# A decoder block on one core: value blocks a weight part later, a latent weight chunk ahead of the queries, the FFN input turned ahead of the last output product

## The chip, the cores and the metric

The kernel runs on one core of a Trainium2 chip. A core has five engines that run side by side, each through its own queue in order: PE (TensorE, matmuls and transposes into PSUM), DVE (VectorE), ACT (ScalarE), POOL (GpSimd) and SP (SyncE, which here issues nearly all loads). The metric is the device time of one execution in microseconds, as a median of several.

## What is computed

One block of a transformer: two token mixers side by side, then a feed-forward network (FFN), for 512 tokens of width 1024, all float32. The reference, cut to what matters:

```python
mod = silu(c) @ ada_w + ada_b                      # six rows of 1024: shifts, scales, gates
h = rms_norm(x, norm1_gain) * (1 + sc1) + sh1
z = h @ w_in                                       # 1024 -> latents, q, k/v of three branches, gates
c_q, c_kv, k_pe, q_n, k_c, v_c, k_s, v_s, k_w, v_w, g_nsa, g_mla, g_merge = split(z)
q  = rms_norm(c_q) @ w_q_b;  kv = rms_norm(c_kv) @ w_kv_b        # latent attention, 8 heads
y_mla = causal_attention(q, k, v) @ w_o_mla
# sparse attention: keys and values of 31 overlapping blocks of 32 tokens,
# compressed by a small network; selected blocks; a window of 256
def compress(t, pos_emb, w1, w2):
    flat = (t[:, blk_idx] + pos_emb).reshape(..., CMP_LEN * Dh)
    return silu(flat @ w1) @ w2
kc, vc = compress(k_c, ...), compress(v_c, ...)
y_nsa = (gated sum of compressed, selected and window attention) @ w_o_nsa
x = x + gt1 * ((sigmoid(g_mla) * y_mla + sigmoid(g_merge) * y_nsa) @ w_out)
h2 = rms_norm(x, norm2_gain) * (1 + sc2) + sh2
x = x + gt2 * ((silu(h2 @ ffn_w_gate) * (h2 @ ffn_w_up)) @ ffn_w_down)
```

## The kernel before

Every product of float32 values is made of three matmuls on halves: a value `v` is split into a rounded high part (`..hi`, `..h`) and the rest (`..lo`, `..l`), and `hi*hi + hi*lo + lo*hi` is summed in PSUM. ACT makes the high half (`hi_of`), DVE the low one (`lo_of`). So each loaded weight chunk (`raw`, loaded by SP) becomes `whi` on ACT, then `wlo` on DVE, and then feeds PE. The pool `wp` has four buffers each of `raw`, `whi` and `wlo`. In PSUM there are four buffers `mm` for sums, two `sc` and two `tp` (transposes and small results).

All engines are wrapped in `Paced`, whose line 153 issues nearly every instruction; that is why the trace gives L153 almost everywhere and instructions are told apart by their tiles. Three things set the order. While `Paced.strict` is true (from line 514 to 1233) every instruction of an engine follows the one written before it, so the written order is the order on the chip. Behind that, a scheduler orders the instructions by its own plan of times, within the dependences. And `gate` on a wrapped engine ties what is issued to follow a given earlier instruction of that engine.

The work goes through these stages, with their times in the trace: modulation strips and the first products (0 to 60 us), the strict part with the rest of `w_in` up to the latents (60 to 148), sparse attention (to 292), latent projections (to 340), latent attention (to 430), gated output products (to 456), the out product `wo` (to 502), the FFN (to 864).

Many steps are generators; `steps(g, n)` runs the next n pieces of one, `run(g)` all of it, `mix` interleaves several by their numbers of pieces, and `with_side` runs one while filler work (gate products, modulation sums) is issued at its side. Three places are touched.

*Lines 1179 to 1201, strict.* `feed.prep(n)` splits the weight chunks up to number n and issues loads four further. `cols_products(j)` multiplies all four token tiles by two of the eight k rows of a part of 352 columns (24 matmuls `ga`); four of these calls make a group, and `keep_cols` copies the group's four sums to `zA`, tiles 0 and 2 on ACT, 1 and 3 on DVE. The next group's sums need the PSUM buffers that these copies free. Between them stand: `blocks["v"]` (`compress_blocks`, line 854), which transposes the value columns `ZC` into `pt`, copies them to `X` (three copies on ACT, one on DVE) and makes, in two halves, `FF` (DVE), its high part `FS` (ACT) and its low part `FS` (DVE); `w1["v"]` (`compress_w1`), four pieces of products `ph` from `FS`; the key side's `nk`, `pk`, `outs["k"]` (`po`, `kcr`, `kcd`, `KH`, `KL`); and `mods_gen` (`mods`, line 1000), pieces of a sum over strips of `ada_w`: a strip is loaded into a single buffer `strip`, and two DVE instructions add its two rows into `macc`.

*Line 1532.* The queries' first half is made token tile by token tile (`tok_major`, tiles `gq`), each tile's result copied to `qn` and squared into `jq` on ACT (`use_q`), and mixed with `kv_chunk(1)`, the load and split of the second chunk of `mla_w_kv_b`, which the products `gk` behind it need.

*Lines 1765 to 1767.* `out_pairs` makes the out product's last two pairs of token tiles in ten pieces; in the second five, `make_h2(0)` is mixed, which scales the first two token tiles to `xs`, and then for each pair of k rows transposes them into `pt`, makes `h2h`, `h2f` and `h2l` (the FFN's input, halves). The FFN's first products `fg` (gate) and `fu` (up) need these; `first_gate_up` goes on with the second half, `make_h2(1)`.

Of the kernel before, what the change touches and what calls it, by code (L numbers as in the profile page):

```python
# [116 lines left out]
def hybrid_block(ctx, tc, a, out):  # L117
# [47 lines left out]
    pe, act, dve, pool, sp = (Paced(e) for e in (nc.tensor, nc.scalar, nc.vector, nc.gpsimd, nc.sync))  # L165
# [149 lines left out]
    def run(gen):  # L315
        for _ in gen:
            pass

    def steps(gen, n):
        for _ in range(n):  # L320
            if next(gen, "end") == "end":
                break
# [20 lines left out]
    def mix(*pairs):  # L343
        todo = [[g, n, 0] for g, n in pairs if n]
        while todo:
            best = min(todo, key=lambda e: (e[2] + 0.5) / e[1])
            if next(best[0], "end") == "end":
                todo.remove(best)
            else:
                best[2] += 1  # L350
                yield
# [18 lines left out]
    def with_side(gen):  # L370
        for _ in gen:
            side.tick()
# [220 lines left out]
    def hA(k, t):  # L593
        return hT[k][0][:, t * P : (t + 1) * P], hT[k][1][:, t * P : (t + 1) * P]
# [20 lines left out]
    def use_q(t, ps):  # L615
        act.activation(out=UQ[t].rearrange("p h d -> p (h d)"), in_=ps, func=AF.Copy)
# [441 lines left out]
    mods_gen = mods()  # L1058
# [4 lines left out]
    blocks, w1, w2, outs = ({nm: f(i, nm) for i, nm in (K, V)} for f in (compress_blocks, compress_w1, compress_w2, compress_out))  # L1063
# [87 lines left out]
    def cols_products(j):  # L1151
        h, l = feed.take(order.index(cols_a[j]))
        if j % 4 == 0:
            gemm["ps"] = [mm.tile([P, S], F32, name=f"ga{t}", tag="mm")[:, :352] for t in range(NT)]
        for i in range(2):
            k = 2 * (j % 4) + i
            for t in range(NT):
                ah, al = hA(k, t)
                o = gemm["ps"][t]
                pe.matmul(o, ah, h[:, i, :], start=(k == 0), stop=False)  # L1160
                pe.matmul(o, ah, l[:, i, :], start=False, stop=False)
                pe.matmul(o, al, h[:, i, :], start=False, stop=(k == KD - 1))

    def keep_cols(j):
        for t in range(NT):
            use_a(352 * j)(t, gemm["ps"][t])
# [12 lines left out]
    steps(outs["k"], 1)  # L1179
    steps(tq, 1)  # L1180
    cols_products(2)
    steps(blocks["v"], 1)
    feed.prep(19)
    steps(blocks["v"], 1)
    steps(mods_gen, 2)
    cols_products(3)
    steps(outs["k"], 1)
    keep_cols(0)
    steps(outs["k"], 1)
    feed.prep(20)  # L1190
    steps(blocks["v"], 1)
    cols_products(4)
    feed.prep(21)
    steps(blocks["v"], 1)
    steps(mods_gen, 2)
# [2 lines left out]
    steps(nk, 1)  # L1198
    steps(w1["v"], 1)
    feed.prep(23)  # L1200
    cols_products(6)
    steps(pk, 1)
    feed.prep(24)
    steps(w1["v"], 1)
# [215 lines left out]
    with tc.tile_pool(name="mp", bufs=1, side="right", reuse_waits="tile") as mp:  # L1420
# [16 lines left out]
        def chunks(w, kt, c0, n, got):  # L1437
            for k0 in range(0, kt, 2):
                got.append(wchunk(rows(a[w][0], k0 * P, 2, c0, n), 2, n))
                yield  # L1440

        def tok_major(off, kt, n, got, consume, tag):
            for t in range(NT):
                ps = mm.tile([P, S], F32, name=f"g{tag}{t}", tag="mm")[:, :n]
                for k in range(kt):
                    ah, al = (v[:, t * P : (t + 1) * P] for v in cT[off + k])
                    h, l = (v[:, k % 2, :] for v in got[k // 2])
                    pe.matmul(ps, ah, h, start=(k == 0), stop=False)
                    pe.matmul(ps, ah, l, start=False, stop=False)
                    pe.matmul(ps, al, h, start=False, stop=(k == kt - 1))  # L1450
                    if k % 3 == 2:
                        yield
                consume(t, ps)
                yield

        wk, wq = [[], []], [[], []]
        kv_chunk = lambda c: chunks("mla_w_kv_b", 2, 512 * c, 512, wk[c])
# [37 lines left out]
        def norm_q(c):  # L1495
            hs = slice(4 * c, 4 * c + 4)
            dve.scalar_tensor_tensor(out=msq[:, c], in0=msq[:, c], scalar=1.0 / MQK, in1=each_t(vq, 4), op0=ALU.mult, op1=ALU.add)
            rsqrt(flat(rsq[:, c]), flat(msq[:, c]), mt, f"q{c}", pool)
            yield
# [29 lines left out]
        za_st.close()  # L1529
        qk_st = scope()  # L1530
        qkp = qk_st.enter_context(tc.tile_pool(name="qkp", bufs=2, reuse_waits="tile"))
        with_side(mix((tok_major(0, 6, 384, wq[0], use_q(0), "q0"), 12), (kv_chunk(1), 1)))
        run(norm_q(0))
        with_side(mix((tok_major(6, 2, 512, wk[1], use_kv(1), "k1"), 4), (q_chunks(1), 3)))
        qk = [[] for _ in range(NH)]
# [225 lines left out]
    wo = gemm_tok(mA, a["w_out"][0], KD, 0, S, use_o(0), tag="wo0")  # L1761
# [2 lines left out]
    run(mix((wo, 6), (as_filler(part(mods_gen, W_MODS)), W_MODS)))  # L1764
    wo = out_pairs()
    steps(wo, 5)
    run(mix((wo, 5), (make_h2(0), 5)))
    mid = {}
    wg, wu, wd = a["ffn_w_gate"][0], a["ffn_w_up"][0], a["ffn_w_down"][0]
    GU = (("g", wg), ("u", wu))  # L1770
# [276 lines left out]
```

## Time and profile before

| | us |
|---|---|
| median of three runs | 867.97 |
| lowest and highest | 866.01, 869.56 |
| the profiled execution | 865.76 |
| its span in the trace | 864.0 |
| PE busy | 838.2 (97%) |
| DVE busy | 674.1 (78%) |
| ACT busy | 455.5 (53%) |
| POOL busy | 108.9 (13%) |

The profile is one execution. Busy time says which engine is full; a list of waits says how long an engine stood still and for whom; a timeline gives each instruction's start and length, and in brackets the time in which the engine stood still before it and what released it. A row `x4` is four instructions of one form in a row, with the length of all. Of a product `out<-in` the names are the tiles'. A matmul's length overlaps the next one's: the distance of two starts is what counts.

### The profile page before, as it was taken

The numbers are of one execution on the slowest core, as the hardware profiler recorded it, in microseconds if no ns is written. First come the engines' busy times: TensorE is split into PE (matmuls) and PEld (weight loads), VectorE is DVE, ScalarE is ACT, GpSimd is POOL, SyncE is SP. The second block draws the span as 40 slices with busy tenths as digits, with TensorE's granted clock in tenths as the row PEclk, the third lists the DMA queues.
The fourth block names the chain that finished last, engine by engine and source line by source line (L and its number), as shares of the span: only waits on it lengthen the run. The fifth ranks groups of instructions, "written<-read, shape, count | busy, mean of one in ns | idle before, by whom it ended". The sixth has DMA issues, their size and how long they took to land.

```text
span 864.0 us, 13969 instructions
## 1 busy us (share of the span) xinstructions
PE 838.2 (97%) x5060; PEld 738.6 (85%) x5060; DVE 674.1 (78%) x1391; ACT 455.5 (53%) x960; POOL 108.9 (13%) x199
## 2 busy tenths in 40 slices
PE   8999999799999999899999999999999999999997
PEld 7889899678777889787888889888999899988996
DVE  5878787888977577779788877975897768966875
ACT  4746645676866576665533264542466236641550
POOL 0007400443431023012200000000000000000000
PEclk9999999899999999999999999999999999999999
DMA  9934555433212134235687644353233413342312
GB/s 309 367 121 141 168 170 145 136 97 86 74 44 61 34 111 131 88 98 177 224 308 259 214 147 146 99 149 104 68 106 114 138 57 103 109 125 79 99 50 98
DMA packets 95705, 115.54 MB, mean 134 GB/s; under 512 B 6564, under 2 KB 68884, under 8 KB 95636
## 3 DMA queue, kind: packets, MB, share of 16 engines
q1 hardware_dynamic: 92596, 108.32, 40.7%
q10 hardware_dynamic: 2400, 4.23, 1.3%
q0 software_dynamic: 640, 2.10, 0.6%
q8 instruction: 40, 0.66, 0.3%
q14 instruction: 29, 0.24, 0.1%
HBM read 106.24 MB, written 8.39 MB: 133 GB/s over the span
## 4 chain that ended last, share of the span: by engine, by line
PE 75%; DVE 8%; DMA 6%; ACT 3%; issue 3%; POOL 2%; SPq 1%; ACTq 0%; POOLq 0%
PE d L153 14%; PE fx L153 12%; PE fy L153 9%; PE gp L153 8%; PE pt L153 4%; PE av L153 3%; PE gwo L153 3%; PE fg L153 3%; PE gym L153 3%; PE fu L153 3%; PE yn L153 3%; PE wo L153 3%; PE gq L153 2%; DMA raw<-in_w_in_dram 2%; DMA araw<-in_ada_w_dram 2%
## 5 line engine op out<-in xcount | busy, mean ns | idle before, releaser
L153 ACT ACTIVATE whi<-raw 128x1024 fp32r<-128x1024 f32 (+4 forms) x159 | 141.0, 905 | 127.2 <-PE d L153 43.7
L153 DVE TENSOR_TENSOR wlo<-raw,whi 128x1024 fp32r<-128x1024 f32 (+4 forms) x140 | 150.8, 1086 | 54.3 <-ACT whi L153 50.3
L153 PE MATMUL d<-wlo,mh 128*128 128x512 f32 (+1 forms) x180 | 70.2, 390 | 0.0
L153 PE MATMUL d<-whi,mh 128*128 128x512 f32 (+1 forms) x180 | 69.6, 391 | 0.6 <-DVE tm L153 0.5
L153 PE MATMUL d<-whi,ml 128*128 128x512 f32 (+1 forms) x180 | 67.3, 389 | 0.0
L153 ACT ACTIVATE s<-s,mn 128x384 f32<-128x384 f32 (+3 forms) x96 | 52.5, 547 | 27.0 <-DVE mn L153 26.7
L153 DVE TENSOR_TENSOR plo<-pt,phi 128x512 fp32r<-128x512 f32 (+2 forms) x78 | 46.2, 602 | 18.0 <-ACT phi L153 17.8
L153 ACT ACTIVATE phi<-pt 128x512 fp32r<-128x512 f32 (+2 forms) x78 | 39.9, 525 | 29.2 <-PE pt L153 28.6
L153 PE MATMUL gp<-hTh,whi 128*128 128x512 f32 x128 | 54.2, 424 | 0.5 <-ACT zA L153 0.5
L153 PE MATMUL gp<-hTh,wlo 128*128 128x512 f32 x128 | 51.1, 399 | 0.0
L153 PE MATMUL gp<-hTl,whi 128*128 128x512 f32 x128 | 50.7, 396 | 0.0
L153 ACT ACTIVATE whi<-s 128x1024 fp32r<-128x1024 f32 (+1 forms) x36 | 30.2, 846 | 31.8 <-PE d L153 18.0
L153 PE MATMUL fx<-h2h,whi 128*128 128x256 f32 x144 | 41.3, 286 | 0.0
L153 PEld LDWEIGHTS d<-whi,mh 128*128 128x128 f32 x180 | 33.7, 188 | 8.8 <-DVE tm L153 1.2
L153 PE MATMUL fx<-h2h,wlo 128*128 128x256 f32 x144 | 40.8, 284 | 0.0
L153 PE MATMUL fx<-h2l,whi 128*128 128x256 f32 x144 | 40.8, 283 | 0.0
L153 PEld LDWEIGHTS d<-whi,ml 128*128 128x128 f32 x180 | 33.8, 188 | 7.6
L153 PEld LDWEIGHTS d<-wlo,mh 128*128 128x128 f32 x180 | 33.8, 188 | 7.4
L153 DVE TENSOR_TENSOR wlo<-s,whi 128x1024 fp32r<-128x1024 f32 (+1 forms) x36 | 33.6, 948 | 7.4 <-ACT whi L153 7.4
L153 PE MATMUL pt<-ident,s 128*128 128x128 f32 x232 | 37.4, 278 | 0.1
L153 PEld LDWEIGHTS pt<-ident,s 128*128 128x128 f32 x232 | 28.1, 142 | 7.4 <-issue 2.1
L153 POOL TENSOR_TENSOR wlo<-raw,whi 128x512 fp32r<-128x512 f32 x20 | 25.5, 1299 | 59.7 <-ACT whi L153 59.7
(433 smaller groups left out, 2658.9 us busy)
## 6 DMA issues: line engine op xcount, KB each, us to landing
raw<-in_ada_w_dram SPq DMA_DIRECT2D x23, 512.0 KB, 4.8
raw<-in_ffn_w_gate_dram SPq DMA_DIRECT2D x22, 512.0 KB, 4.0
raw<-in_ffn_w_up_dram SPq DMA_DIRECT2D x22, 512.0 KB, 4.0
raw<-in_ffn_w_down_dram SPq DMA_DIRECT2D x22, 512.0 KB, 3.8
araw<-in_ada_w_dram SPq DMA_DIRECT2D x32, 256.0 KB, 6.5
raw<-in_w_in_dram SPq DMA_DIRECT2D x16, 512.0 KB, 4.4
strip<-in_ada_w_dram SPq DMA_DIRECT2D x9, 512.0 KB, 3.9
raw<-in_w_in_dram SPq DMA_DIRECT2D x12, 352.0 KB, 3.3
```

What stands on the lines that cost most here:

```text
L153: out = call(*args, **kw)
```

## The change

The computation and the instructions stay; their order changes in three places. In the strict part, the value blocks' first two pieces (transposes, copies) go from ahead of the fourth part to behind it and behind the fifth, their halves go correspondingly later, and two pieces of the modulation sums that stood ahead of the fourth part now stand ahead of the seventh. The second `mla_w_kv_b` chunk is loaded and split whole before the queries, with gates on ACT and DVE. And the pieces of `make_h2(0)` are written out between those of the out product's last part, so that its transposes stand ahead of the last twelve matmuls.

```diff
--- before.py
+++ after.py
@@ -1179,17 +1179,15 @@
     steps(outs["k"], 1)
     steps(tq, 1)
     cols_products(2)
-    steps(blocks["v"], 1)
     feed.prep(19)
-    steps(blocks["v"], 1)
-    steps(mods_gen, 2)
     cols_products(3)
     steps(outs["k"], 1)
     keep_cols(0)
     steps(outs["k"], 1)
+    steps(blocks["v"], 1)
     feed.prep(20)
+    cols_products(4)
     steps(blocks["v"], 1)
-    cols_products(4)
     feed.prep(21)
     steps(blocks["v"], 1)
     steps(mods_gen, 2)
@@ -1198,7 +1196,9 @@
     steps(nk, 1)
     steps(w1["v"], 1)
     feed.prep(23)
+    steps(mods_gen, 2)
     cols_products(6)
+    steps(blocks["v"], 1)
     steps(pk, 1)
     feed.prep(24)
     steps(w1["v"], 1)
@@ -1529,7 +1529,10 @@
         za_st.close()
         qk_st = scope()
         qkp = qk_st.enter_context(tc.tile_pool(name="qkp", bufs=2, reuse_waits="tile"))
-        with_side(mix((tok_major(0, 6, 384, wq[0], use_q(0), "q0"), 12), (kv_chunk(1), 1)))
+        run(kv_chunk(1))
+        act.gate, dve.gate = act.last, dve.last
+        with_side(tok_major(0, 6, 384, wq[0], use_q(0), "q0"))
+        act.gate = dve.gate = None
         run(norm_q(0))
         with_side(mix((tok_major(6, 2, 512, wk[1], use_kv(1), "k1"), 4), (q_chunks(1), 3)))
         qk = [[] for _ in range(NH)]
@@ -1764,7 +1767,16 @@
     run(mix((wo, 6), (as_filler(part(mods_gen, W_MODS)), W_MODS)))
     wo = out_pairs()
     steps(wo, 5)
-    run(mix((wo, 5), (make_h2(0), 5)))
+    first_h2 = make_h2(0)
+    steps(first_h2, 1)
+    steps(wo, 3)
+    steps(first_h2, 1)
+    pe.gate = pe.last
+    steps(wo, 1)
+    steps(first_h2, 1)
+    steps(wo, 1)
+    pe.gate = None
+    run(first_h2)
     mid = {}
     wg, wu, wd = a["ffn_w_gate"][0], a["ffn_w_up"][0], a["ffn_w_down"][0]
     GU = (("g", wg), ("u", wu))
```

On DVE, from the fourth latent part on. Here `X_1` and `FF` belong to the value blocks, `zA_794` and `zA_796` are the copies of tiles 1 and 3, `macc` the sums, `KL` the compressed keys. Before:

```order
L153 COPY X_1_1441<-pt 64x511
L153 TENSOR_SCALAR macc<-strip,csil 128x512
L153 SCALAR_TENSOR_TENSOR macc<-strip,csil,macc 128x512
L153 COPY zA_794<-ga_1287 128x352
L153 COPY zA_796<-ga_1289 128x352
L153 TENSOR_TENSOR KL<-pt,KH 128x2x32 x2
L153 TENSOR_TENSOR wlo<-raw,whi 128x704
L153 TENSOR_TENSOR FF_1503<-X_1_1441,cols_778 128x8x32 x2
L153 TENSOR_TENSOR FS_1502<-FF_1503,FS_1502 128x8x64
L153 TENSOR_TENSOR wlo<-raw,whi 128x1024
L153 TENSOR_TENSOR FF_1542<-X_1_1441,cols_778 128x8x32 x2
L153 TENSOR_TENSOR FS_1502<-FF_1542,FS_1502 128x8x64
```

and now:

```order
L153 COPY zA_794<-ga_1287 128x352
L153 COPY zA_796<-ga_1289 128x352
L153 TENSOR_TENSOR KL<-pt,KH 128x2x32 x2
L153 TENSOR_TENSOR wlo<-raw,whi 128x704
L153 COPY X_1_1481<-pt 64x511
L153 TENSOR_TENSOR wlo<-raw,whi 128x1024
L153 TENSOR_TENSOR FF_1533<-X_1_1481,cols_778 128x8x32 x2
L153 TENSOR_TENSOR FS_1532<-FF_1533,FS_1532 128x8x64
L153 TENSOR_SCALAR macc<-strip,csil 128x512
L153 SCALAR_TENSOR_TENSOR macc<-strip,csil,macc 128x512
```

The copies of `zA` and `KL` come first, then `X`, and the first pair of sums stands behind the first `FS`; the second `FF` is some twenty rows further.

On ACT, at the queries: `cTh` is the last turned latent, `qn` and `jq` are a query tile's copy and squares, `whi 128x1024` is the second `mla_w_kv_b` chunk and the `128x768` ones are the queries' next chunks. Before:

```order
L153 ACTIVATE cTh_3801<-pt,cols_778 128x512
L153 ACTIVATE qn_3574<-gq_3809 128x384
L153 ACTIVATE jq,msq<-gq_3809 128x96 x4
L153 ACTIVATE qn_3575<-gq_3839 128x384
L153 ACTIVATE jq,msq<-gq_3839 128x96 x4
L153 ACTIVATE qn_3576<-gq_3875 128x384
L153 ACTIVATE jq,msq<-gq_3875 128x96 x3
L153 ACTIVATE whi<-raw 128x1024
L153 ACTIVATE jq,msq<-gq_3875 128x96
L153 ACTIVATE whi<-raw 128x768
```

and now:

```order
L153 ACTIVATE cTh_3801<-pt,cols_778 128x512
L153 ACTIVATE whi<-raw 128x1024
L153 ACTIVATE qn_3574<-gq_3815 128x384
L153 ACTIVATE jq,msq<-gq_3815 128x96 x4
L153 ACTIVATE qn_3575<-gq_3845 128x384
L153 ACTIVATE jq,msq<-gq_3845 128x96 x4
L153 ACTIVATE qn_3576<-gq_3875 128x384
L153 ACTIVATE qn_3577<-gq_3905 128x384
L153 ACTIVATE whi<-raw 128x768 x2
L153 ACTIVATE jq,msq<-gq_3875 128x96 x4
```

The chunk's split went from behind the third tile's squares to ahead of the first tile's copy, and the squares of the third tile went behind two further splits.

On PE, at the second token half of the FFN's input, whose transposes are the rows `pt<-ident,xs`; `h2h_5539` to `h2l_5554` are the eight k rows' halves, both token halves in one tile. Before:

```order
L153 MATMUL fg_5986<-h2l_5554,whi 128x256
L153 MATMUL pt<-ident,xs 128x128
L153 MATMUL fg_5986<-h2h_5553,wlo 128x256
L153 MATMUL fg_5987<-h2h_5553,whi 128x256
L153 MATMUL pt<-ident,xs 128x128 x3
L153 MATMUL fg_5987<-h2l_5554,whi 128x256
L153 MATMUL fg_5987<-h2h_5553,wlo 128x256
L153 MATMUL pt<-ident,xs 128x128 x4
L153 MATMUL fu_5989<-h2h_5547,wlo 128x256
L153 MATMUL fu_5988<-h2h_5549,whi 128x256
L153 MATMUL fu_5988<-h2l_5550,whi 128x256
L153 MATMUL fu_5988<-h2h_5549,wlo 128x256
```

and now:

```order
L153 MATMUL fu_5989<-h2l_5554,whi 128x256
L153 MATMUL fu_5989<-h2h_5553,wlo 128x256
L153 MATMUL pt<-ident,xs 128x128 x8
L153 MATMUL fg_5986<-h2h_5539,whi 128x256
L153 MATMUL fg_5987<-h2h_5539,whi 128x256
L153 MATMUL fu_5988<-h2h_5539,whi 128x256
L153 MATMUL fu_5989<-h2h_5539,whi 128x256
L153 MATMUL pt<-ident,xs 128x128 x4
L153 MATMUL fg_5986<-h2l_5540,whi 128x256
```

Before, the eight transposes stand among the first half's matmuls; now they follow the last of these, and the second half's own products (`h2h_5539` again) follow them directly.

## Rows read from the trace of the kernel before

**Rows 1.** The page's first part: engine, busy us, share of the span, instructions.

```profile
PE 838.2 (97%) x5060; PEld 738.6 (85%) x5060; DVE 674.1 (78%) x1391; ACT 455.5 (53%) x960; POOL 108.9 (13%) x199
```

**Rows 2.** Waits of PE over the span: who waited <- for whom, us, times, longest.

```profile
PE pw L153 <- DVE mn L153: 5.1, 5, 3.1
```

**Rows 3.** Timeline of PE, 102 to 130: start, length, instruction, [wait before it].

```profile
103.65 0.66 PE L153 MATMUL pt<-ident,ZC 128*128 128x128 f32 x4 [1.12 <-DVE kcr L153]
...
110.60 0.43 PE L153 MATMUL ga<-whi,hTh 128*128 128x352 f32 x1 [0.88 <-DVE zA L153]
...
117.38 0.28 PE L153 MATMUL ph<-whi,FS 128*128 128x256 f32 x1
...
129.39 0.43 PE L153 MATMUL ga<-whi,hTh 128*128 128x352 f32 x1
```

**Rows 4.** The same, PE at 318 to 320.

```profile
318.47 0.97 PE L153 MATMUL gk<-whi,cTh 128*128 128x512 f32 x3 [0.60 <-ACT whi L153]
...
319.84 0.50 PE L153 MATMUL gk<-wlo,cTh 128*128 128x512 f32 x1 [0.40 <-DVE wlo L153]
```

**Rows 5.** The same, PE at 501 to 516.

```profile
501.85 0.39 PE L153 MATMUL wo<-whi,mTl 128*128 128x512 f32 x1
...
503.84 0.50 PE L153 MATMUL fg<-h2h,whi 128*128 128x256 f32 x2 [0.73 <-ACT h2h L153]
...
505.47 0.38 PE L153 MATMUL fg<-h2l,whi 128*128 128x256 f32 x1 [0.89 <-DVE h2l L153]
...
515.62 0.60 PE L153 MATMUL pt<-ident,xs 128*128 128x128 f32 x4
```

**Rows 6.** The same, ACT at 106.

```profile
106.15 1.80 ACT L153 ACTIVATE X<-pt 64x512 f32<-64x512 f32 x3 [2.54 <-POOL X L153]
```

**Rows 7.** The same, DVE, 106 to 130.

```profile
106.16 1.23 DVE L153 TENSOR_TENSOR wlo<-raw,whi 128x1024 fp32r<-128x1024 f32 x1
...
107.99 0.69 DVE L153 COPY X<-pt 64x511 f32<-64x511 f32 x1 [0.61 <-ACT X L153]
...
112.89 1.09 DVE L153 TENSOR_TENSOR FF<-X,cols 128x256 f32<-128x256 f32 x2
...
114.67 0.69 DVE L153 TENSOR_TENSOR FS<-FF,FS 128x512 fp32r<-128x512 f32 x1 [0.70 <-ACT FS L153]
...
119.17 1.53 DVE L153 SCALAR_TENSOR_TENSOR macc<-strip,csil,macc 128x512 f32<-128x512 f32 x2
...
128.82 0.95 DVE L153 COPY zA<-ga 128x352 f32<-128x352 f32 x2
```

**Rows 8.** One stretch: busy us of PE, PEld, DVE, ACT, POOL, then clock, DMA share, GB/s.

```profile
106.16:129.77 23.61, 22.58 (x146) 21.69 (x145) 20.09 (x40) 11.31 (x19) 0.00 (x0) 1.00 0.54 158
```

**Rows 9.** The page's sixth part: DMAs of one form, KB each, us to landing.

```profile
strip<-in_ada_w_dram SPq DMA_DIRECT2D x9, 512.0 KB, 3.9
```

**Rows 10.** Timeline of ACT, 308 to 318.

```profile
313.68 0.49 ACT L153 ACTIVATE qn<-gq 128x384 f32<-128x384 f32 x1 [5.66 <-PE gq L153]
...
317.26 1.16 ACT L153 ACTIVATE whi<-raw 128x1024 fp32r<-128x1024 f32 x1
```

**Rows 11.** The same, ACT at 497.

```profile
497.65 1.14 ACT L153 ACTIVATE xs<-x,r 128x1024 f32<-128x1024 f32 x1
```

**Rows 12.** The same, PE at 155.

```profile
155.73 0.31 PE L153 MATMUL pw<-KH,QS 128*128 128x160 f32 x1 [3.09 <-DVE mn L153]
```

**Rows 13.** The same, DVE at 151.

```profile
151.42 3.07 DVE L153 TENSOR_TENSOR kpr<-zA,g_k 128x32 f32<-128x32 f32 x3
```

**Rows 14.** Stretches again; the granted clock of PE is the third number from the end.

```profile
100.00:112.00 12.00, 9.85 (x60) 8.92 (x60) 10.05 (x30) 5.86 (x13) 5.65 (x17) 1.00 0.44 125
...
155.00:160.00 5.00, 4.27 (x18) 3.77 (x18) 3.23 (x20) 2.64 (x12) 1.52 (x4) 0.68 0.74 217
...
160.00:165.00 5.00, 3.43 (x18) 2.62 (x18) 4.83 (x27) 3.02 (x14) 1.40 (x4) 0.84 0.78 202
```

**Rows 15.** Timeline of POOL at 149.

```profile
149.26 5.18 POOL L153 TENSOR_TENSOR wlo<-raw,whi 128x512 fp32r<-128x512 f32 x4 [43.14 <-ACT whi L153]
```

## The prediction

> **What bounds the kernel now.** I read the page's table of engines first: TensorE (PE) is busy 838.2 us of the 864.0 us span [rows 1]. A reordering adds and removes no matmul, so all it can win is the 26 us in which PE stands still, and it wins only the waits it reaches. So the second view is PE's list of waits: the longest entry is the scores `pw` waiting for the row minima `mn`, 5.1 us in five waits [rows 2]. The third view is the timeline of PE and of the engines that feed it at the three places that the diff edits. Before edit 1's products, PE waits 1.12 us for `kcr` and 0.88 us for VectorE's (DVE's) `zA` copies [rows 3]. At the second latent weight chunk it waits 0.60 us for `whi` and 0.40 us for `wlo` [rows 4]. At the start of the FFN it waits 0.73 us for `h2h` and 0.89 us for `h2l` [rows 5]. Together the three edits aim at 2.00 + 1.00 + 1.62 = 4.6 us, half a per cent of the span. About 0.5% (4.3 us) is also the least that a measurement of this kernel can tell from no change.
>
> **Edit 1, value blocks and sums later.** The four `ZC` transposes stood ahead of the fourth latent part; they waited because their PSUM buffer still held the key side's result until DVE had read it into `kcr`. Now they stand behind that part, so it starts at once, 1.12 us earlier. The `X` copies and two sums no longer stand ahead of DVE's `zA` copies, so the 0.88 us goes too: PE arrives at the first value product about 2.0 us before its old 117.38 [rows 3], at 115.4, or a little sooner.
>
> What is late next? That product reads `FS`, and its whole chain now begins later. ScalarE (ACT) copies three quarters of `X` in 1.80 us [rows 6], now only behind its own `zA` copies and one weight split, so I put them at 109.7 to 111.5. DVE then copies its `X` (0.69), splits a weight (1.23), and goes from `FF` to the end of `FS` as before in 115.36 - 112.89 = 2.47 us [rows 7]: 111.5 + 0.3 (handing over) + 0.69 + 1.23 + 2.47 = 116.2. PE waits about 0.8 us there, and 1.2 us of the lead is left.
>
> The rest is DVE's. In the ninth part (second `zA` group) the third tile starts at 129.39 [rows 3], right after DVE's first copy of that group, 128.82 plus half of 0.95 = 129.30 [rows 7]: it already came just in time. Between the weight split at 106.16 and the end of those copies DVE does the same set of instructions before and after, 20.09 us of work in 23.61 us [rows 7, 8], and the split at 106.16 itself hangs on the unmoved `kcr` work. After the first `FS` (116.2) and a pair of sums (at most 1.53, so 117.7), of the 20.09 us about 11.2 is left up to the first copy's end (what now lies ahead of that point, three splits, `zA`, `KL`, `X`, `FF`, `FS` and the sums, is about 8.4, and 0.48 is the second copy), and one more wait for ACT's half of `FS`, 0.7 like the 0.70 ahead of the first [rows 7]. That gives 129.6. Beside it runs a second chain: the strip buffer is single, and each strip takes 3.9 us to land [rows 9] after the sums that read the one before: 117.7 + 3.9 + 1.53 + 3.9 + 1.53 + 0.48 = 129.0. Both ends lie within 0.3 us of the old 129.30; I take +0.2 us, DVE's being the later one (129.6 is +0.3, the mean of both +0.0). So the lead of 1.2 us is spent as a new wait in the ninth part. Bounds: if DVE's 3.5 us of idle time closed up instead, the whole 2.0 us would stay (-2.0); if the first sums came one more split (1.23) later, every strip behind them would be as much later (+0.2 + 1.2 = +1.4). On SP's queue the strips moved behind weight and compress loads; four weight buffers lie ahead of PE, and none of the loads has a wait in PE's list, so that costs nothing beside the strip chain itself.
>
> **Edit 2, second latent chunk ahead of the queries.** ACT stands idle for 5.66 us up to 313.68, then does the queries' squares, and only at 317.26 the split `whi` (1.16 us); DVE's `wlo` after that [rows 4, 10]. Now `whi` is ahead of the first query copy, inside that idle time, and DVE's `wlo` can follow between the query rows, before PE wants it. PE arrives at about 317.9 (318.47 - 0.60), so both waits go: -1.0. In exchange ACT does the squares of two query tiles behind the next splits, which releases the third `gk` tile's PSUM about 0.1 us late: +0.1. Sum -0.9; bounds -1.0 and +0.5 (the query copies and their PSUM wait on ACT by half a split).
>
> **Edit 3, FFN input ahead of the last product.** The scaled input `xs` is ready at 497.65 + 1.14 = 498.79 [rows 11]; the first four transposes now run twelve matmuls of 0.23 us before the end of the output product (last start 501.85, so at 499.3) [rows 5], and `h2h` and `h2l` are made beside those matmuls: 2.8 us of cover against 1.62 of waiting. The 0.73 and 0.89 go: -1.62. But the scheduler also lays out the first FFN products anew. Before, the second token half's eight transposes stand between matmuls of the first half (the last four at 515.62) and nothing waits [rows 5]. Now all eight stand in a row behind the last of them, and the next `fg` needs their `h2h` at once. That is the arrangement of 502 again, where two waits came of it, but with ACT and DVE free beforehand; I take 0.3 for `h2h` and 0.4 for the next transposes' buffer, and as bounds nothing and the old 1.62 (then +0.9 with the losses ahead). Sum -0.9, between -1.6 and +0.9.
>
> **What moves along.** The order of the sparse attention from 165 to 292 us changes too, since the scheduler plans it anew. PE has little to lose or win there: of the 5.1 us, one wait of 3.09 at 155.73 is ahead of the first moved row [rows 12], and the other four make 2.0 together. I take 0; bounds -2.0 (these gone) and +3.1 (one more wait as long as the longest).
>
> **The sum.** +0.2 - 0.9 - 0.9 + 0 = -1.6 us. The profiled execution took 865.76 us, 2.2 us less than the median of 867.97, so it would be 864.2 there and 866.4 as a median.
>
> **Rivals.** *The early lead stays.* DVE's idle time closes up and edit 1 gives -2.0: 867.97 - 2.0 - 1.8 = 864.2. For it speaks that DVE is idle 3.5 of 23.6 us [rows 8]; against it, that it is idle in handovers with ACT, which the new order has as many of.
>
> *Slower, by a starved PE in the sparse attention.* At 155.73 PE waits 3.09 us because DVE was held in three small products `kpr`, 3.07 us [rows 12, 13]; and after it the granted clock is 0.68 and 0.84 of 2.4 GHz for five microseconds each, that is, part of the time at 1.2 GHz [rows 14]. If the new order puts another such run ahead of scores, it costs 3.1 + (0.32 + 0.16) x 5 = 5.5 us: 866.4 + 5.5 = 871.9. It decides from the wait's length: after the 1.12 us wait at 103.65 the clock stayed at 1.00 [rows 14], after 3.09 it didn't. The Trainium skill ("TensorE: Matmul & The Clock Gate", section "HAM oscillation — how this bites in real kernels") says the same, that idle gaps between bursts send the clock to half; the trace agrees with its 0.68. Against this rival: DVE's rows there are mostly shorter ones and the moved rows are only regrouped.
>
> *Faster, by the same place the other way.* ScalarE's and GpSimd's (POOL's) rows in 148 to 156 are ordered as before, but they start from other times. POOL's four weight splits (5.18 us from 149.26) lie beside the slow `kpr` [rows 13, 15]. If they come apart, the wait and its clock go: 866.4 - 5.5 = 860.9. The Trainium skill ("SBUF — State Buffer", section "SBUF: two separate sides") makes this a rule: a DVE instruction with two SBUF inputs and a reading GpSimd instruction lock each other out. By it the three `kpr` would shrink wherever POOL is idle; the rows fit it, but no row shows a `kpr` without POOL. Against the rival: what POOL and DVE wait for there, the gate weights and the last `zA` copies, moves by the same few tenths.
>
> *Edits 2 and 3 change nothing in sum.* The waits only change place (ACT's squares, the second half's transposes), and edit 1's +0.2 is left: 867.97 + 0.2 = 868.2. That the change wouldn't do what it says is excluded by the order of instructions: the moved rows stand where the diff puts them.
>
> **How the numbers follow.** My forecast (866.4, within some 1.5 us) 0.45; the lead stays 0.17; edits 2 and 3 net nothing 0.18; slower by starvation 0.11; faster at 155 us 0.09. The first three lie within 0.5% (863.6 to 872.3) with their values; a fifth of the lead's cases lie below it, most of the faster rival's, and of the slower one's about half lie above, with a little of the rest. So faster by over 0.5% 0.11, same 0.82, slower 0.07. The range leaves out the faster rival and the upper half of the slower one: 862.4 to 870.2.
>
> **What would show it.** In the changed kernel's trace: no wait of `pt` for `kcr`; the first value product `ph` at 116 to 116.5 after a wait for `FS`; a wait of 1 us or so for `zA` in the ninth part and its third tile at 129.4 to 130; `gk` without waits for `whi` and `wlo`; `fg` without waits at 502, and one or two of a few tenths behind the second half's transposes near 514. Edit 1 is misjudged if the third tile comes at 128 or earlier, or if macc waits on a strip for over 1 us; edit 2, if `gk` waits for ACT; edit 3, if the second half's waits reach 1.6. The forecast is wrong in its last term if the span from 165 to 292 grows or shrinks by over 2 us.

## The result, and the profile after

| | before | after |
|---|---|---|
| median, us (6 runs each, side by side) | 868.19 | 874.55 |
| lowest and highest | 866.01, 869.56 | 871.63, 875.66 |
| the profiled execution | 865.76 | 874.95 |
| its span | 864.0 | 873.2 |

The changed kernel is slower: ratio 1.0066, 95% interval 1.0047 to 1.0084, 5.7 us for a central value. The prediction said 866.4 us, no measurable change, and its range ended at 870.2. It was wrong, and on the side of the rival "slower, by a starved PE in the sparse attention".

The page's table of engines for the kernel after, engine, busy us, share of the span, instructions, to be read against [rows 1]:

```profile
PE 844.7 (97%) x5060; PEld 741.7 (85%) x5060; DVE 674.8 (77%) x1391; ACT 455.8 (52%) x960; POOL 109.4 (13%) x199
```

The instructions are the same in number, and the busy times of DVE, ACT and POOL moved by under 1 us. PE is 9.2 us longer on its way and counts 6.5 us more as busy; a busy PE is not PE at its peak, so this table can't say where the time went. The list of PE's waits in the kernel after (who waits for whom, us, times, longest):

```profile
PE pw L153 <- DVE mn L153: 4.6, 5, 3.1
PE ps L153 <- DVE mn L153: 4.3, 8, 1.1
...
PE gk L153 <- ACT jq L153: 1.7, 2, 1.4
PE ga L153 <- DVE zA L153: 1.3, 1, 1.3
PE ph L153 <- DVE FS L153: 1.0, 1, 1.0
```

Its first entry is about as before [rows 2]. The second has grown; before, it was:

```profile
PE ps L153 <- DVE mn L153: 2.4, 5, 0.8
```

New are `gk` for `jq` (edit 2's place) and `ph` for `FS` (edit 1's), and `ga` for `zA` grew from 0.9 to 1.3. But others went, and all waits of this list together grow from 21.2 to 23.5 us: 2.3 of the 9.2.

What finds the rest is a comparison of landmarks: the start of the same PE instruction in both traces, and how the difference grows along the program.

| place, time before | difference, us |
|---|---|
| end of the strict part, first `gp`, 148.35 | +0.6 |
| first value product `av`, 167.3 | +1.8 |
| a later `av`, 218 | +2.2 |
| next `av`, 227 | +8.3 |
| first `gk`, 297.6 | +7.2 |
| last `gk` of the latent stage, 323 | +7.9 |
| first `av` of the latent attention, 361 | +8.6 |
| the same, 410 | +10.3 |
| FFN, 525 | +9.4 |
| FFN, 580 and later | +9.2 |

Five of the 9.2 us arise in one stretch of the sparse attention, between 216 and 228 us, where no edit was made (+6.1 there, of which 1.1 comes back up to 298). The three edited places give +0.6, +1.4 (with what follows in the latent stage) and -0.9. The remaining differences, +1.2 ahead of 167 and +1.7 between 395 and 410, stand where TensorE's granted clock is lower than in the trace of before; that is in the last section.

**The stretch.** The sparse attention works through eight units, a token tile and a head group each: sixteen score products (`pw`, `ps`), then the softmax on DVE, ACT and POOL, then transposes of the weights (`pt` from `cm`, then from `s`) and value products `av`. Between them PE gets filler work, the gate products `gp`. Scores run ahead, beside the unit before. DVE masks each score (`s`) and takes its minimum (`mn`), `sm` are the softmax's sums, `cm` its weights on the compressed blocks. For the fifth unit, two rows of PE before (the unit's last pair of score products, the first of its transposes) and one of DVE (the softmax's last step ahead of that transpose):

```profile
207.81 0.34 PE L153 MATMUL ps<-KH,QS 128*128 128x384 f32 x1
...
217.25 0.60 PE L153 MATMUL pt<-ident,cm 128*32 128x128 f32 x4
```

```profile
213.32 0.29 DVE L153 TENSOR_TENSOR cm<-cm,sm 128x128 f32<-128x128 f32 x1
```

The softmax takes 213.6 - 207.8 = 5.8 us, and PE comes for its result 3.6 us later. The same unit in the kernel after, PE (from its last score on), then DVE:

```profile
219.44 0.34 PE L153 MATMUL ps<-KH,QS 128*128 128x384 f32 x1
...
222.06 0.42 PE L153 MATMUL pw<-KH,QS 128*128 128x416 f32 x1 [0.28 <-DVE mn L153]
...
223.64 0.43 PE L153 MATMUL pw<-KH,QS 128*128 128x416 f32 x1 [0.51 <-DVE sm L153]
...
224.63 0.44 PE L153 MATMUL ps<-KH,QS 128*128 128x384 f32 x1 [0.37 <-DVE mn L153]
...
225.11 0.61 PE L153 MATMUL pt<-ident,cm 128*32 128x128 f32 x4
...
226.75 0.65 PE L153 MATMUL pt<-ident,s 128*128 128x128 f32 x2 [0.32 <-DVE s L153]
...
227.75 0.50 PE L153 MATMUL gp<-hTh,whi 128*128 128x512 f32 x1
```

```profile
219.99 0.62 DVE L153 CUSTOM_DVE_ANT_0 s<-ps,mask,rs_n 128x384 f32<-128x384 f32 x1
...
222.44 0.22 DVE L153 RECIPROCAL sm<-sm 128x12 f32<-128x12 f32 x1
...
222.88 0.61 DVE L153 CUSTOM_DVE_ANT_0 s<-pw,consts,rs_n 128x384 f32<-128x384 f32 x1
...
223.41 0.17 DVE L153 TENSOR_TENSOR sm<-sm,gn 128x12 f32<-128x12 f32 x1
...
223.96 0.60 DVE L153 CUSTOM_DVE_ANT_0 s<-ps,mask,rs_n 128x384 f32<-128x384 f32 x1
...
224.50 0.56 DVE L153 TENSOR_TENSOR cm<-cm,sm 128x128 f32<-128x128 f32 x1
224.99 2.03 DVE L153 TENSOR_SCALAR s<-s,sm 128x384 f32<-128x384 f32 x4
```

The softmax takes as long as before, 225.06 - 219.44 = 5.6 us. But the unit's last scores stand 11.6 us later, at the end of the previous unit's values instead of ahead of most of them. Counted in the two traces, 45 products and transposes stand between that pair and the transposes of `cm` before, 22 of them fillers, and 15 after, one of them a filler. Twelve of the 15 are scores that already belong to the next unit; each needs a buffer that DVE frees, and DVE puts their masks (222.88, 223.96) between the steps of the chain PE waits for. From 219.44 to the next filler at 227.75 PE has 14 score products, four products of 512 columns and two groups of transposes: by the distances of their starts in the trace before (0.185, 0.23 and 0.36 us) 2.6 + 0.9 + 0.7 = 4.2 us of work in 8.3 us. So 4.1 us are lost here, 2.4 up to the transposes of `cm` and 1.7 behind them, where the transposes of `s` come as DVE scales each (224.99). The waits with a name are 1.74 of the 4.1. The rest shows as no idle time at all: a product that stands alone counts 0.34 to 0.50 us as busy, where the starts of a full stream are 0.185 to 0.23 apart. Two windows show it, of before and of after; columns as in [rows 8]:

```profile
217.00:225.00 8.00, 8.00 (x41) 6.03 (x40) 6.74 (x28) 7.86 (x23) 2.63 (x3) 1.00 0.31 98
```

```profile
220.00:228.00 8.00, 6.26 (x25) 3.35 (x24) 7.98 (x31) 6.45 (x22) 3.08 (x5) 1.00 0.22 80
```

41 matmuls before, 25 after, and DVE full in after (7.98 of 8.00). The granted clock is 1.00 in both.

Why does the scheduler not put fillers there? The kernel ties each one: `Paced.pace`, 16 in this stage (`PACE_D`), makes a `gp` follow the sixteenth last product of the attention *as written*. So a filler can run ahead of at most fifteen of the attention's products, and the scores of the next unit aren't tied. That this tie kept the fillers out is read from the code; no run shows it.

### The profile page after: what moved, and what is told of

It reads as the page before. It is cut to its first block, busy times and chain, and to the rows that moved or that the text cites. A ratio compares the mean times of both kernels' runs of the same rounds, so it can differ in the third digit from the quotient of the medians.

```text
span 873.2 us, 13961 instructions
## 1 busy us (share of the span) xinstructions
PE 844.7 (97%) x5060; PEld 741.7 (85%) x5060; DVE 674.8 (77%) x1391; ACT 455.8 (52%) x960; POOL 109.4 (13%) x199
## 4 chain that ended last, share of the span: by engine, by line
PE 78%; DVE 9%; DMA 6%; ACT 3%; issue 2%; SPq 1%; POOL 0%; ACTq 0%; DVEq 0%
PE d L153 14%; PE fx L153 12%; PE fy L153 9%; PE gp L153 8%; PE pt L153 4%; PE av L153 3%; PE yn L153 3%; PE wo L153 3%; PE gwo L153 3%; PE gym L153 3%; PE fg L153 3%; PE fu L153 3%; PE ga L153 2%; PE gq L153 2%; DMA araw<-in_ada_w_dram 2%; DVE wlo L153 2%
```

## The experiments

All were run beside the kernel before, in five rounds each; its medians were 869.25, 868.0 and 868.3 us in the three sets. "Pinned" means that in the sparse attention each instruction of every queue follows the one that stands before it in a recorded order, so the scheduler has no choice there.

| run | median, us | ratio to before | 95% interval |
|---|---|---|---|
| edit1_only | 876.11 | 1.0075 | 1.0053 to 1.0097 |
| edit1_sparse_pinned | 868.69 | 0.9999 | 0.9985 to 1.0013 |
| sparse_swapped | 874.1 | 1.0063 | 1.0038 to 1.0089 |
| edit2_only | 870.09 | 1.0028 | 1.0013 to 1.0043 |
| edit2_squares_first | 868.6 | 1.0013 | 1.0000 to 1.0025 |
| edit3_only | 866.06 | 0.9979 | 0.9960 to 0.9997 |
| all_sparse_pinned | 868.56 | 1.0010 | 0.9997 to 1.0022 |
| stretch_filled | 873.52 | 1.0054 | 1.0036 to 1.0073 |
| kpr_late | 863.79 | 0.9953 | 0.9936 to 0.9969 |
| edit3_kpr_late | 861.52 | 0.9921 | 0.9901 to 0.9942 |

**Is it edit 1 itself, or the order that it sets off?** Three runs: edit 1 alone, which is the first two pieces of the diff; edit 1 with the sparse attention pinned to the order of the kernel before; and the kernel before, without any edit, pinned to the order of the kernel after. The pin, behind the sparse attention's code:

```diff
+    for e, runs in zip((pe, act, dve, pool, sp), PIN):
+        seq = [pinned[e][a + i] for a, n in runs for i in range(n)]
+        for p, q in zip(seq, seq[1:]):
+            pe.follow(q, p)
```

`edit1_only`. 

> Edit 1 alone (value blocks and sums later). Theory O, the order: edit 1 alone makes the scheduler lay out the sparse attention anew, and that order costs; +0.5 us at the end of the strict part and about +6.6 between 148 and 304 us, as in the changed kernel, so +6 to +8 us (ratio 1.007 to 1.009), with scores of unit (t=2, g=1) standing without filler gp for some 7 us. Theory C, the clock: the cost is that PE arrives half a microsecond later at a clock that falls near 155 us; then the same +4 to +6 here, but by a lower granted clock alone. Theory E, the edits behind it: the loss comes from edits 2 and 3 as well; then here +1 to +3.

`edit1_sparse_pinned`. 

> Edit 1 as above, and the sparse attention's instructions tied into the order that they have in the kernel before (on all five queues). Theory O: only edit 1's own +0.2 to +0.6 us is left (ratio 1.000 to 1.001). Theory C: the later arrival is still there, so +4 to +6 us.

`sparse_swapped`. 

> The kernel before with none of the edits, but its sparse attention tied into the order of the changed kernel. Theory O: +5 to +7 us (ratio 1.006 to 1.008), with the same bare stretch of scores. Theory C: the arrival is that of before, so within +1 us.

Measured: edit 1 alone costs 0.75%; with the old order it costs nothing (-0.1 us, interval -1.3 to +1.1); and the new order without any edit costs 0.63% (5.5 us, interval 3.3 to 7.7). In `sparse_swapped` the landmarks jump from +1.6 to +7.2 at the same place as in the kernel after, through waits of the same length. The clock is no rival: the mean granted clock of the six executions of `sparse_swapped` is 0.991 and that of the 21 of before 0.992. So the loss belongs to the order of the sparse attention, in which not a line of the diff stands; that edit 1 moved the times from which the scheduler plans is the likely way to it. The pin ties all five queues, so the runs don't say which queue's order costs.

**Can fillers in the stretch mend it?** In `sparse_swapped`, nine `gp` that stand behind the fifth unit's transposes were put among its neighbours' scores, with the pace off (the order is pinned anyway). On PE:

```diff
 pw<-KH,QS_791
 pw<-KL,QS_791
+gp x3
 ps<-KH,QS_791
 ps<-KL,QS_791
+gp x3
 pw<-KH,QS_790
 pw<-KL,QS_790
+gp x3
 ps<-KH,QS_790
 ps<-KL,QS_790
...
 av<-phi,VC
-gp x9
```

> The kernel before, without the three edits, its sparse attention in the order of the kernel after on all queues (as in the run sparse_swapped, 874.1 us, ratio 1.0063 to before), with one thing changed: nine gate products (gp) that stood behind the transposes of unit (2, 1) now stand between that unit's scores, three behind each of the second, third and fourth group of two score products; the filler's pace, which ties a gate product to the sixteenth last product of the attention, is off in this stage so that they may stand there. Theory 'unfilled scores': the stretch of some 7.5 us costs because PE has only the scores there and waits 1.74 us in the rows (0.28, 0.51, 0.37, 0.26, 0.32) and about 1.5 us more in gaps too short for a row; nine products of 0.23 us, 2.1 us in all, fill waits and stand no longer behind the transposes: 1.5 to 2.1 us faster than sparse_swapped, a ratio to before of about 1.004, and the landmarks after 226 us stand 1.5 to 2.1 us earlier than in sparse_swapped. Rival 'the softmax chain sets the stretch': the products push the scores back, the transposes behind them come as much later, and less than 0.5 us is gained: ratio 1.006.

The windows of `sparse_swapped`, then of `stretch_filled`, over the stretch and behind it (columns as above: PE's busy time comes right after the window's length, the granted clock is the third from the end):

```profile
220.00:228.00 8.00, 6.23 (x25) 3.31 (x24) 7.97 (x31) 6.45 (x21) 2.83 (x5) 1.00 0.19 67
228.00:238.00 10.00, 10.00 (x49) 7.78 (x49) 9.42 (x31) 6.58 (x19) 3.44 (x4) 1.00 0.17 50
```

```profile
220.00:228.00 8.00, 7.28 (x34) 5.18 (x33) 7.94 (x33) 6.78 (x23) 3.86 (x4) 1.00 0.20 66
228.00:238.00 10.00, 9.26 (x41) 7.35 (x40) 9.71 (x31) 6.06 (x17) 4.20 (x6) 0.83 0.25 73
```

The nine fillers fit in: 34 matmuls instead of 25 in the same 8 us. This run comes to the stretch 0.31 us ahead of `sparse_swapped`, and its transposes of `cm` stand 0.24 us behind; first `sparse_swapped`, then `stretch_filled`:

```profile
224.86 0.61 PE L153 MATMUL pt<-ident,cm 128*32 128x128 f32 x4
```

```profile
225.10 0.60 PE L153 MATMUL pt<-ident,cm 128*32 128x128 f32 x4
```

So 2.1 us of fillers cost the transposes 0.55. Behind them the values `av` stand 1.5 us ahead at 230, a gain of 1.2. Up to 233 all of it goes: there the fillers are missing (41 matmuls instead of 49), PE waits for the next unit's `phi` and `plo`, and the clock is 0.83, which is 0.17 x 10 = 1.7 us. From 248 us on the landmarks stand 0.3 us ahead again, as in front of the stretch, and the FFN, planned a little differently, loses some 0.3.

By the medians neither theory is settled: the interval, 1.0036 to 1.0073, holds both forecasts, 1.004 and 1.006. The granted clocks say more. The span of the 61 executions of before is 0.78 us longer for each microsecond lost at the lower clock (span times one minus the granted clock). The six executions here lost 8.6 us so and those of `sparse_swapped` 7.6; by this estimate the fillers save some 2.1 us (1.2 to 3.0) at equal clock, as the first theory had it, and 0.8 of that goes to the clock. The rest of the order's cost, over 3 us, they don't mend. What is left to explain it is how far ahead of its transposes a unit's last score stands. That is read from the two orders; no run moved that score alone. The count of matmuls by itself gives no price: the third unit has 18 in place of 47 in the new order and PE waits 0.77 us for its `cm`, the fourth 24 in place of 63, and yet the landmarks of the kernel after go from +1.8 at 167 us to +1.0 at 199.

**Edit 2 alone, and with the squares first.** The second kernel adds a gate which holds the queries' next two splits behind the squares `jq`:

```diff
     norm_q(0)
+    act.gate = act.last
     with_side(mix((tok_major(6, 2, 512, wk[1], use_kv(1), "k1"), 4), (q_chunks(1), 3)))
+    act.gate = None
```

`edit2_only`. 

> Edit 2 alone (second latent chunk ahead of the queries). My prediction's term was -0.9 us. By the trace of the changed kernel, gk waits 0.33 and 1.39 us for ACT's jq instead of 0.60 and 0.40 for whi and wlo: +0.7 us (ratio 1.001).

`edit2_squares_first`. 

> Edit 2 with one more gate: on ACT, what belongs to the next key rows and query chunks follows the last squares of the query tiles. If the gk waits come from the two splits that stand ahead of these squares, they shrink to 0.3 or less: -0.7 us against before (ratio 0.999), 1.4 us less than edit 2 alone. If ACT is late at gk anyway, as edit 2 alone.

Edit 2 costs 2.4 us (interval 1.1 to 3.7); its trace shows 1.4 of it between 320 and 361 us. ACT in the kernel after, then PE:

```profile
322.97 1.06 ACT L153 ACTIVATE whi<-raw 128x1024 fp32r<-128x1024 f32 x1 [7.77 <-PE gq L153]
323.93 0.47 ACT L153 ACTIVATE qn<-gq 128x384 f32<-128x384 f32 x1
...
327.19 1.67 ACT L153 ACTIVATE whi<-raw 128x768 fp32r<-128x768 f32 x2
328.67 0.33 ACT L153 ACTIVATE jq<-gq 128x96 f32<-128x96 f32 x1
```

```profile
325.38 0.50 PE L153 MATMUL gk<-whi,cTh 128*128 128x512 f32 x1 [0.33 <-ACT jq L153]
...
329.84 0.50 PE L153 MATMUL gk<-whi,cTh 128*128 128x512 f32 x1 [1.39 <-ACT jq L153]
```

The split does stand ahead of the queries' copies, but not inside ACT's old idle time: that time is now 7.77 us long, and a `gq` ends it (what the split needs of that product no row says). On before's clock (7.2 us less) the split starts at 315.8, 1.5 us earlier than at 317.26, and the first copy `qn` at 316.7, 3.0 us later than at 313.68 [rows 10]. Everything that ACT does on the queries is that much later. Then the third tile's squares also stand behind two splits of 1.67 us together, and `gk` needs the PSUM buffer that they read: 1.39 us. In place of 0.60 + 0.40 us [rows 4] PE waits 0.33 + 1.39. With the squares first, PE's waits in this stretch are:

```profile
319.24 0.50 PE L153 MATMUL gk<-whi,cTh 128*128 128x512 f32 x1 [0.33 <-ACT jq L153]
326.49 0.44 PE L153 MATMUL gq<-whi,cTh 128*128 128x384 f32 x1 [1.19 <-DVE VM L153]
```

The second `gk` wait is gone, as expected, and a wait of `gq` for `VM` takes its place behind it. The price is 1.1 us (0 to 2.2), not the expected gain of 0.7. Against edit 2 alone, twelve executions of each in one set and both at a mean granted clock of 0.992, it is 1.5 us less (0.2 to 2.9 by the means; 1.4 was expected). So the squares behind the two splits are a good part of edit 2's cost, and edit 2 gains nothing in either form.

**Edit 3 alone**, the last piece of the diff.

> Edit 3 alone (FFN input ahead of the last output product). My prediction's term: -0.9 us (ratio 0.999), the waits of 0.73 and 0.89 at 502 gone and about 0.7 of new ones at the second token half. The rival, that they only change place: 0. Theory E has the loss partly here: +1 or more.

It gains 1.8 us (interval 0.3 to 3.5). Its landmarks go from +0.3 ahead of the edit (498 us) to -0.6 at 525 and -0.7 behind 580. The waits at [rows 5] are gone; what is left at the second token half is, in the kernel after:

```profile
526.95 0.50 PE L153 MATMUL fg<-h2h,whi 128*128 128x256 f32 x2 [0.33 <-ACT h2h L153]
528.13 0.66 PE L153 MATMUL pt<-ident,xs 128*128 128x128 f32 x4 [0.43 <-ACT h2f L153]
```

**All three edits in the old order.**

> All three edits, and the sparse attention tied into the order of before. Theory O (the whole loss is the sparse order): what is left is edit 1's 0, edit 2's, edit 3's -1.8 us, so -2.5 to -0.5 us (ratio 0.997 to 0.999). If something else of the change costs too (edit 2's wait for jq, 0.7 us in the changed kernel, or a lower clock behind it), 0 to +2.

868.56 us, ratio 1.0010: the whole change without the new sparse order is no measurable change. It isn't the gain of 0.5 to 2.5 us that theory O had, since edit 2 costs. The parts add up: the order +5.5, edit 1 -0.1, edit 2 +2.4, edit 3 -1.8, together +6.0 against the +5.7 of the ratio; each part is known to 1.2 to 2.2 us.

**The slow `kpr` at 155 us.** The rival "faster, by the same place the other way" rested on three `kpr` beside POOL's splits. In the kernel before, pinned to its own order, the four `kpr` products of DVE and the four operations of POOL that follow them went to the end of the stage. On DVE:

```diff
-kpr<-zA_793,g_k
 cm<-pw,rs_n,consts
...
-kpr<-zA_795,g_k
-kpr<-zA_794,g_k
-kpr<-zA_796,g_k
 macc<-raw,csil,macc
...
 of<-of,av
+kpr<-zA_793,g_k
+kpr<-zA_795,g_k
+kpr<-zA_794,g_k
+kpr<-zA_796,g_k
 plo<-pt,phi
```

> The kernel before, its sparse attention tied into its own order, but the four products kpr on DVE and the four POOL instructions behind them are moved to the end of it. Theory: at 155 us the scores wait 3.09 us for mn because DVE is held 3.07 us by three kpr beside POOL's weight splits, and the granted clock falls after it. Then the wait goes (or shrinks below 1 us), kpr takes 0.2 to 0.4 us each where POOL is idle, and the clock stays at 1.00 there: -3 to -6 us (ratio 0.993 to 0.997). Rival: PE then waits there for the next thing (POOL's splits or a strip from memory), and the gain is under 1 us.

Before, as a group by line, and in this run (the numbers are the shortest, middle and longest in ns, then the first and last start):

```profile
L153 DVE TENSOR_TENSOR kpr<-zA,g_k x4: 624/1286/1307, 149.5 to 153.2; 128x32 f32<-128x32 f32 x4
```

```profile
L153 DVE TENSOR_TENSOR kpr<-zA,g_k x4: 176/176/177, 278.0 to 278.3; 128x32 f32<-128x32 f32 x4
```

PE's longest wait for scores in this run:

```profile
157.00 0.31 PE L153 MATMUL pw<-KH,QS 128*128 128x160 f32 x1 [0.91 <-DVE mn L153]
```

A `kpr` without POOL beside it takes 176 ns instead of 1286, and PE's waits for `mn` in 155 to 165 us are 0.91, 0.42, 0.29 and 0.37 us in place of 3.09 [rows 12], 0.31, 0.42, 0.29 and 0.56. The kernel gains 4.1 us (2.7 to 5.6). But the expected clock of 1.00 did not come in this trace, whose windows are

```profile
155.00:160.00 5.00, 3.03 (x15) 2.27 (x15) 4.41 (x25) 2.97 (x14) 0.37 (x1) 0.83 0.97 263
160.00:165.00 5.00, 4.97 (x18) 3.93 (x18) 3.99 (x18) 3.52 (x11) 3.01 (x6) 0.50 0.15 54
```

against 0.68 and 0.84 before [rows 14]. This trace and that of before have the same granted clock over the whole span, 0.996, and their landmarks end 2.4 us apart. The six executions lost 3.7 us at the lower clock on average, the 29 of before in their set 6.4, so the rest of the 4.1 us goes with a clock that fell for less time.

Before, each slow `kpr` was as long as one of POOL's four splits (5.18 / 4 = 1.30 us [rows 15]). The Trainium skill ("SBUF — State Buffer", section "SBUF: two separate sides") says that a DVE operation with two SBUF inputs and a GpSimd operation that reads SBUF hold their shared port for a whole instruction each; by that a `kpr` waits out one split, and the 1286 and 176 ns agree with it.

**The best version.** Edit 3 and the late `kpr`, in the sparse order of the kernel before.

> The kernel before with edit 3 alone, its sparse attention in the order of the kernel before on all queues but for the eight operations on kpr (four on VectorE, four on GpSimd), which stand at the stage's end. Theory 'independent stages': edit 3 alone measured 1.8 us faster and kpr late alone 4.2 us faster; they lie 350 us apart and share no wait, so 6 us faster than before, some 862 us, ratio 0.993. Rival 'the gain is given back' (the later stages are bound by a transfer or another engine that does not start earlier): about 863.8 us as kpr late alone, ratio 0.995.

861.52 us, ratio 0.9921 (0.9901 to 0.9942), 6.9 us faster than before (5.0 to 8.6): the two gains, 1.8 and 4.1, add up within the interval, and this beats both kernels.

## Why the prediction was wrong, point by point

**What bounds the kernel.** "All it can win is the 26 us in which PE stands still" was sound for what can be won. For what can be lost it says nothing: that PE has no wait at a place means that the order there covers the latencies, not that any order does. That 0.5% is the least that can be told was too much: edit 3's 0.21% was told.

**Edit 1: right.** The forecast was +0.2 us, -0.1 was measured. Its steps can be read in the kernel after: no wait for `kcr`, `ph` at 116.19 after 0.98 us for `FS` (forecast: 116 to 116.5 after 0.8), and a third tile of the ninth part at 129.98 after 1.30 us for `zA` (forecast: 129.4 to 130 after about 1):

```profile
116.19 0.38 PE L153 MATMUL ph<-whi,FS 128*128 128x256 f32 x1 [0.98 <-DVE FS L153]
129.98 0.43 PE L153 MATMUL ga<-whi,hTh 128*128 128x352 f32 x1 [1.30 <-DVE zA L153]
```

The lead was won and spent, as argued. In `edit1_sparse_pinned` the fourth part starts 2.0 us ahead of before's, the lead is 2.7 at most, and from the third tile of the ninth part on the run stands 0.3 behind.

**Edit 2: the term mis-sized, with the wrong sign.** -0.9 was forecast with an upper bound of +0.5; +2.4 was measured. The step that failed is "Now `whi` is ahead of the first query copy, inside that idle time". ACT's idle time was not free for the split: the split waits for a `gq` too, 2.1 us longer than the first copy did, and the gate then holds the copies behind it. The listing showed the two splits ahead of the third tile's squares; I put the squares' delay at 0.1 us, from no row, where the two splits' own 1.67 us stood.

**Edit 3: right.** -0.9 was forecast, -1.8 (-3.5 to -0.3) measured; by the landmarks from 498 to 525 us it is -0.9 in the trace of the kernel after and in that of edit 3 alone, and -0.2 more behind. The two new waits were put at 0.3 and 0.4 us and measured 0.33 and 0.43; no row stood behind these two values, so that they came so close is luck.

**The sparse attention: the step that failed.** "PE has little to lose or win there ... I take 0; bounds -2.0 and +3.1" became +5.5. I drew the bound from the waits of the old order, one more wait as long as the longest. The sign that the prediction named for its own error, a span from 165 to 292 us that grows by over 2 us, came: it grew by 5.3. But the loss did not come as a long wait; it came in a stretch where PE had half its work, as five waits of 0.26 to 0.51 us and as products that stood alone. The rival that named the place had the wrong mechanism too (a run of small DVE products with the clock falling after it): no such run stands there, and the clock in the stretch stayed at 1.00. That its price, 5.5 us, is the one measured is luck: it was made of a wait of 3.1 and 2.4 of clock. "The moved rows are only regrouped" was no argument, since a regrouping can change the distance between a result and its use. The order of instructions could have raised the question before any run: the matmuls between each unit's last score and its first transpose could be counted, 45 before and 15 after in the fifth unit.

**The sum.** With edit 2 at +2.4 in place of -0.9 the forecast would have been 866.4 + 3.3 = 869.7, within the range. The order's 5.5 us alone, 866.4 + 5.5 = 871.9, put the result outside it.

## What to carry to other kernels

Where a scheduler plans part of a program, an edit ahead of that part can replan it, and the replanned part has to be costed like an edit: count, in the two orders, the bound engine's work between each result and its use, and hold it against the latency the old trace shows (here 5.8 us of softmax against 15 matmuls). The count says where to look, not what it costs. To judge an edit by itself, pin everything else to the old order; half a per cent of accidental order hid that of three edits one gains, one costs and one does nothing that can be measured. And idle time of an engine is only room for a moved instruction if that instruction's own inputs and buffers are there when the idle time begins.

## What was not expected of the hardware

**The clock falls in some executions and not in others, after waits of like length.** A wait at the same place in the latent attention, in the trace of before and of after (PE, then the two windows from there on):

```profile
396.73 0.44 PE L153 MATMUL ps<-kh,qh 96*128 96x384 f32 x1 [0.84 <-DVE mn L153]
...
395.00:400.00 5.00, 3.88 (x24) 2.95 (x23) 4.22 (x9) 2.96 (x8) 0.60 (x1) 1.00 0.46 134
400.00:405.00 5.00, 5.00 (x29) 4.24 (x28) 4.39 (x11) 3.15 (x9) 1.94 (x3) 1.00 0.66 193
```

```profile
405.52 0.44 PE L153 MATMUL ps<-kh,qh 96*128 96x384 f32 x1 [1.03 <-DVE mn L153]
...
405.00:410.00 5.00, 4.20 (x15) 3.26 (x16) 4.94 (x12) 3.06 (x9) 0.60 (x1) 0.75 0.62 191
410.00:415.00 5.00, 5.00 (x26) 4.14 (x25) 3.82 (x10) 2.65 (x7) 2.52 (x3) 0.91 0.41 141
```

After 0.84 us the clock stayed at 2.4 GHz; after 1.03 it was at 1.2 GHz for part of the next ten microseconds, which costs 0.25 x 5 + 0.09 x 5 = 1.7 us. The prediction's "it decides from the wait's length", between 1.12 and 3.09 us, is too simple: 1.12 us at 103.65 left the clock at 1.00 [rows 3, 14], 1.03 here did not. At 154 to 170 us the clock falls in every trace, for different lengths: 3.4 us lost before, 6.8 after, 1.7 in `all_sparse_pinned` up to 160 and 5.1 more up to 174, and 3.4 in `kpr_late`, whose longest wait there is 0.91 us. In the twelve traces the granted clock over the whole execution lay between 0.987 and 0.996, so between 11.3 and 3.4 us were lost. A microsecond lost need not cost one: by the 61 executions of before it costs 0.78 (0.69 to 0.87; an estimate, since a granted clock is noted to 0.001, which is 0.9 us), and the 3.4 us more that the trace of after lost at 154 to 170 moved its landmarks by 1.2. So two profiles of one kernel can differ by several microseconds from this alone. Of the 9.2 us between the two traces, 2.9 stand where the clock is lower (1.2 and 1.7), and medians of runs had to decide: the mean granted clock is 0.9925 over the six executions after and 0.9921 over 61 of before.
